# The FFN's up-projection in two Strassen parts: 512 tokens as before, then 2 x 1024 tokens through half-size products of 512 columns

## The chip, the core and the metric

The kernel runs on one core of one Trainium2 chip. A core has five engines, each with an instruction queue of its own that is worked off in order: TensorE (PE in the profile; its weight loads PEld), VectorE (DVE), ScalarE (ACT), GpSimd (POOL) and SyncE (SP, which here issues nearly all DMAs). They meet through semaphores. On-chip data lie in SBUF, matmuls write to PSUM, which has eight banks of 128 x 512 f32. The metric is the device time of one execution in microseconds, the median of several runs.

## The reference, cut

One layer of a bidirectional encoder in f32, for two batches with the same weights: a sample S of 2048 tokens and a prompt P of 512.

```
h = RMSNorm(x); p = h @ w_in
A: windowed attention   B: centred pooling   C: Hyena (FFT convolution)
x = x + concat(RMSNorm_A(a), RMSNorm_B(b), RMSNorm_C(c)) @ w_out
x = x + ConvGLU(RMSNorm(x)):
    u = h @ w_ffn_in                 # 1024 -> 2 x 2816
    u = depthwise conv of width 3 along the tokens + bias
    x += (gelu(u[:2816]) * u[2816:]) @ w_ffn_out
```

The change is in the first line of the ConvGLU, and in what is put beside it.

## The kernel before, in words

Each f32 product is made of three matmuls of rounded parts: `split` (L316) makes a high part on ACT (L318) and the rest on DVE (L319), and `mm3` (L321) multiplies high with high, high with low, low with high into one PSUM bank (L323, L324, L325). Activations are kept transposed, with features on the partitions, so the moving operand of the up-projection is 512 tokens of normed input (`h`, or `hp` for P) and the stationary one a 128 x 128 piece of weights (`fwhi`, `fwlo`).

`run` (L1433) builds the program from two generators at a time: `drive` takes steps of a main chain and of a side chain in a ratio of their estimated PE costs. That fixes each engine's order, up to a list scheduler beneath that keeps every engine's queue in order of readiness as it models it. The side chain is one sequence: mixers of S (spectra, pooling, Hyena, attention), the normed and transposed input of S's first half (`norm_s`), then, once the main chain has begun the up-projection (`need("up")`), attention, pooling, Hyena and output projection of P, and `prep_p`, P's normed input. Main chain: the input projections and S's output projection (`front`), then

- `ffn_in(S, hA, 0, 1024)`, beside the side chain at `RATIO_P` = 0.4,
- `ffn_in(P, hp, 0, 512)`, beside `ffn_prep` of S's second half,
- `ffn_in(S, hB, 1024, 1024)`, beside the first eight weight tiles of the down-projection (`load`),
- `ffn_out`, which reads the products back from DRAM and loads the other 14 weight tiles.

`ffn_in` (L1286) goes over 22 feature tiles x 2 parts (gate and up). Per tile: a 512 KB weight load (`fw`, two buffers), its split (ACT and DVE, 1024 columns each), then 8 k x 3 matmuls per 512 tokens, an ACT copy with tap 1 and bias from PSUM (L1322), two DVE taps from PSUM (L1312), and at the gate a Gelu (L1338). DVE multiplies gate and up (L1340), SP stores the 128 rows (`acts`, `actp`). `ffn_prep` loads 128 tokens (`nx`, two buffers), takes Square with a sum on ACT (L343), the power -1/2 on POOL (L346), the scaling on DVE (L347), eight PE transposes (L357), and splits them from PSUM on ACT and DVE (L360, L361).

Of the kernel before, what the change touches and what calls it, by code (L numbers as in the profile page):

```python
# [18 lines left out]
DM = 1024  # L19
# [13 lines left out]
class Seq:  # L33
    """One request batch: its length, its FFT split N = 64 * N2 and the derived tile counts."""
# [15 lines left out]
# the tables of 128 partitions that stay on chip: name and columns  # L50
# [5 lines left out]
def _shape_tables():  # L56
    """DFT matrices, positions, decays, distances: all from shapes alone."""
# [40 lines left out]
    # of the first four heads; those of the others are 1/16 of it  # L98
# [14 lines left out]
    for s in SEQS.values():  # L113
# [34 lines left out]
        # rows (b, ri, g, j), columns (ri, g, k2), block diagonal over g  # L148
# [13 lines left out]
        # positions of the forward filter and of the backward one, in the order (j, b, n1)  # L162
# [15 lines left out]
        # [b, n1, chunk, g, j, c']  # L178
# [15 lines left out]
def _arrays(inputs):  # L194
    """The arrays of the launch: the large inputs as they are, the small ones laid out by partition."""
# [35 lines left out]
RATIO_P = 0.4  # L231
# [10 lines left out]
class Trunk:  # L242
    def __init__(self, ctx, tc, d):
# [3 lines left out]
        for s in SEQS.values():  # L247
# [6 lines left out]
            self.act[n] = self.dr.tile([D_FF, s.L], F32, name="act" + n)  # L254

    def consts(self, c):
# [12 lines left out]
        self.edge = c.tile([128, 2, 2 * NF], F32, name="edge")  # L269
# [46 lines left out]
    def split(self, x, hi, lo):  # L316
        nc = self.nc
        self.keep(nc.scalar.activation(hi, x, AF.Copy))  # L318
        self.keep(nc.vector.tensor_tensor(lo, x, hi, op=ALU.subtract))  # L319

    def mm3(self, ps, lhi, llo, rhi, rlo, start, stop):  # L321
        nc = self.nc
        nc.tensor.matmul(ps, lhsT=lhi, rhs=rhi, start=start, stop=False)  # L323
        nc.tensor.matmul(ps, lhsT=lhi, rhs=rlo, start=False, stop=False)  # L324
        nc.tensor.matmul(ps, lhsT=llo, rhs=rhi, start=False, stop=stop)  # L325

    def row(self, pool, src, name):
        """A vector of DM on every partition."""
# [9 lines left out]
    def norm(self, pool, g, x, n):  # L338
        """The first n rows of x after RMS norm with gain g, in place."""
# [10 lines left out]
    def norm_t(self, xn, n, hi, lo, c0, bank):  # L350
        """xn, transposed, to columns c0.. of hi and lo."""
# [13 lines left out]
    def front(self):  # L365
        """p of the sample, q, k and v of both, p of the prompt, then the sample's output projection behind its attention. The
        weights of a part take the place of those of the part before, tile by tile."""
# [5 lines left out]
        with tc.tile_pool(name="front", bufs=1, reuse_waits="tile") as pool:  # L373
# [16 lines left out]
            def fill(i, c0):  # L390
                """Weights i: columns c0.. of w_in, piece by piece."""
# [30 lines left out]
            def place(i):  # L422
                """Where row tile i goes, transposed: hi, lo and the column."""
# [32 lines left out]
            def also(it):  # L456
                """it, with the row tiles and the weights to come."""
# [54 lines left out]
            # the first tiles as they come; the weights last, for the next pool to start below them  # L512
# [55 lines left out]
            def out_fill(k, dst):  # L568
                """Row tile k of the scaled w_out into dst [128, 2, DM]."""
# [57 lines left out]
            def rest():  # L627
                """The weights to come."""
# [24 lines left out]
    def filt_sin(self, pool, ps, li, x):  # L653
        """sin's argument f * (ps + b) into x, reduced to [-pi, pi]."""
# [905 lines left out]
```

## Time and profile before

| | us |
|---|---|
| median of 3 runs | 3138.26 (3133.56 to 3141.27) |
| span of the profiled execution | 3140.1 |
| first to last up-projection matmul | 1144.9 to 2531.3 |
| of these the stage with P | 1783.8 to 2036.4 |
| landing of a weight tile (`fw`, 512 KB, 132 of them) | 3.8 |
| ACT split of it / DVE split of it | 1.06 / 1.22 |

A row of a group reads: line, engine, operation, out<-in, shapes, count, then busy us and mean ns of one, then the engine's idle time just before and what ended it. A row of a tile gives minimum, median and maximum in ns, then when the first and the last began. A row of a stretch gives begin and end, its length, busy us (and count) of PE, PEld, DVE, ACT and POOL, the granted share of TensorE's clock, the share of the DMA engines and GB/s. A DMA row gives the count, KB each and median us from issue to landing. A timeline's row begins with start and duration in us. A matmul's duration of about 0.39 us includes its way through the array: they overlap, and one follows another in about 0.23 us.

### The profile page before, as it was taken

The page shows a single profiled execution, that of the slowest core. Times are in us where ns is not written, and L with a number is a line of the kernel's source. Part 1 is how long each engine was busy: PE and PEld are TensorE (multiplying, and loading weights), DVE is VectorE, ACT ScalarE, POOL GpSimd, SP SyncE. Part 2 cuts the span into 40 slices and gives each one's busy share as a digit, 9 for nine tenths or more (in the row PEclk, how much of TensorE's full clock was granted, in tenths as well). Part 3 has the DMA queues.
Part 4 walks back from the last instruction along what each step waited for, and adds up shares of the span by engine and source line. Part 5 has one row for each costly group of instructions (what it writes and reads, how often), then busy time and mean ns, then how long its engine had stood idle before and what let it go on. Part 6 is the DMA issues. An engine that isn't in the chain of part 4 may idle for free.

```text
span 3140.1 us, 41553 instructions
## 1 busy us (share of the span) xinstructions
PE 3053.5 (97%) x15992; PEld 2556.1 (81%) x15992; DVE 1676.3 (53%) x3168; ACT 1173.7 (37%) x2021; POOL 210.5 (7%) x248
## 2 busy tenths in 40 slices
PE   7999999899999999999999999999999999999999
PEld 6887888888878877788887888888888888888887
DVE  7443567759998777666445565564444442111111
ACT  5222454448877546434223343332222231111110
POOL 1000000012233230000000000000000000000000
PEclk9999999999999999999999999999999999999999
DMA  5555586663533441454313243442222143223222
GB/s 178 151 152 138 163 230 170 178 176 100 152 100 94 145 138 61 131 166 133 98 63 128 89 137 118 127 142 67 74 67 74 54 131 111 74 77 101 74 75 77
DMA packets 399051, 369.94 MB, mean 118 GB/s; under 512 B 74937, under 2 KB 332857, under 8 KB 397829
## 3 DMA queue, kind: packets, MB, share of 16 engines
q1 hardware_dynamic: 395685, 356.64, 37.6%
q0 software_dynamic: 2880, 10.49, 0.8%
q8 instruction: 126, 2.06, 0.3%
q14 instruction: 72, 0.59, 0.1%
q10 hardware_dynamic: 288, 0.16, 0.0%
HBM read 278.08 MB, written 89.13 MB: 117 GB/s over the span
## 4 chain that ended last, share of the span: by engine, by line
PE 69%; DVE 5%; ACT 3%; DMA 2%; issue 1%; POOL 1%; SPq 0%; POOLq 0%; ACTq 0%; DVEq 0%
PE b L323 21%; PE b L325 21%; PE b L324 21%; PE b L1160 1%; PE b L1111 1%; ACT sb L1127 1%; PE b L1142 1%; PE b L1141 1%; PE b L865 1%; PE b L852 1%; DVE sb L1114 0%; PE b L357 0%; DVE nx L347 0%; DVE sb L1135 0%; DMA raw<-in_w_in_dram 0%
## 5 line engine op out<-in xcount | busy, mean ns | idle before, releaser
L323 PE MATMUL b<-h,fwhi 128*128 128x512 f32 x1408 | 562.5, 400 | 0.9 <-DVE x L1237 0.9
L325 PE MATMUL b<-h,fwlo 128*128 128x512 f32 x1408 | 560.0, 398 | 0.3 <-DVE fwlo L319 0.3
L324 PE MATMUL b<-h,fwhi 128*128 128x512 f32 x1408 | 559.0, 397 | 0.0
L1312 DVE SCALAR_TENSOR_TENSOR cv<-b,cst,cv 128x511 f32<-128x511 f32 (+1 forms) x616 | 351.8, 593 | 153.9 <-ACT cv L1322 147.3
L319 DVE TENSOR_TENSOR fwlo<-fw,fwhi 128x1024 fp32r<-128x1024 f32 x132 | 161.4, 1224 | 326.7 <-ACT fwhi L318 326.7
L325 PEld LDWEIGHTS b<-h,fwlo 128*128 128x128 f32 x1408 | 265.5, 189 | 64.5 <-DVE fwlo L319 0.8
L323 PEld LDWEIGHTS b<-h,fwhi 128*128 128x128 f32 x1408 | 265.8, 189 | 63.1 <-issue 1.8
L324 PEld LDWEIGHTS b<-h,fwhi 128*128 128x128 f32 x1408 | 265.7, 189 | 61.6
L319 DVE TENSOR_TENSOR al<-ar,ah 128x512 fp32r<-128x512 f32 x110 | 76.0, 691 | 420.4 <-ACT ah L318 420.4
L318 ACT ACTIVATE fwhi<-fw 128x1024 fp32r<-128x1024 f32 x132 | 139.8, 1059 | 387.9 <-PE b L324 385.1
L324 PE MATMUL b<-h,ah 128*128 128x512 f32 x640 | 249.2, 389 | 0.0
L323 PE MATMUL b<-h,ah 128*128 128x512 f32 x640 | 249.1, 389 | 0.0
L325 PE MATMUL b<-h,al 128*128 128x512 f32 x640 | 248.9, 389 | 0.0
L318 ACT ACTIVATE ah<-ar 128x512 fp32r<-128x512 f32 x110 | 69.4, 631 | 474.9 <-PE b L324 462.4
L1322 ACT ACTIVATE cv<-b,cst 128x512 f32<-128x512 f32 x220 | 169.2, 769 | 200.1 <-PE b L325 199.9
L323 PE MATMUL b<-W,h 128*128 128x256 f32 (+1 forms) x672 | 224.7, 334 | 2.1 <-ACT W L318 0.7
L324 PE MATMUL b<-W,h 128*128 128x256 f32 (+1 forms) x672 | 214.8, 320 | 0.7 <-DVE W L319 0.3
L325 PE MATMUL b<-W,h 128*128 128x256 f32 (+1 forms) x672 | 213.9, 318 | 0.0
L323 PE MATMUL b<-h,W 128*128 128x256 f32 x640 | 200.3, 313 | 3.4 <-ACT W L318 1.5
L325 PE MATMUL b<-h,W 128*128 128x256 f32 x640 | 184.5, 288 | 3.8 <-DVE W L319 3.8
L324 PE MATMUL b<-h,W 128*128 128x256 f32 x640 | 183.1, 286 | 0.0
L325 PEld LDWEIGHTS b<-h,al 128*128 128x128 f32 x640 | 120.1, 188 | 25.3 <-DVE al L319 0.2
(204 smaller groups left out, 5791.8 us busy)
## 6 DMA issues: line engine op xcount, KB each, us to landing
fw<-in_w_ffn_in_dram SPq DMA_DIRECT2D x132, 512.0 KB, 3.8
ar<-acts SPq DMA_DIRECT2D x88, 256.0 KB, 2.7
nx<-in_x_sample_dram SPq DMA_DIRECT2D x32, 512.0 KB, 4.4
tf<-in_t2f_s_dram SPq DMA_DIRECT2D x64, 256.0 KB, 3.3
acts<-cv SPq DMA_DIRECT2D x22, 512.5 KB, 2.6
raw<-in_w_in_dram SPq DMA_DIRECT2D x44, 256.0 KB, 3.1
rw<-in_w_ffn_out_dram SPq DMA_DIRECT2D x44, 256.0 KB, 2.7
acts<-cv SPq DMA_DIRECT2D x22, 511.5 KB, 3.1
```

What stands on the lines that cost most here:

```text
L318: self.keep(nc.scalar.activation(hi, x, AF.Copy))
L319: self.keep(nc.vector.tensor_tensor(lo, x, hi, op=ALU.subtract))
L323: nc.tensor.matmul(ps, lhsT=lhi, rhs=rhi, start=start, stop=False)
L324: nc.tensor.matmul(ps, lhsT=lhi, rhs=rlo, start=False, stop=False)
L325: nc.tensor.matmul(ps, lhsT=llo, rhs=rhi, start=False, stop=stop)
L852: nc.tensor.matmul(ps[:, i * C:i * C + C], lhsT=tf[:, i], rhs=x1[:, k0 + i], start=True, stop=True)
L865: nc.tensor.matmul(ps[:, i * C:i * C + C], lhsT=ti[:, i], rhs=t1[:, i * C:i * C + C], start=True, stop=True)
L1111: nc.tensor.matmul(ps[:, :nk], lhsT=qs[h][:, b * 128:b * 128 + 128], rhs=kk[:, ks], start=(i == 0), stop=(i == 1))
L1127: nc.scalar.activation(sc[h][:, :nk], sc[h][:, :nk], AF.Exp, bias=ng[:, h:h + 1], accum_out=den[:, h:h + 1])
L1141: nc.tensor.matmul(po, lhsT=v, rhs=phi, start=(i == 0), stop=False)
L1312: nc.vector.scalar_tensor_tensor(o, ps, taps[i], o if to is None else to, op0=ALU.mult, op1=ALU.add)
L1322: nc.scalar.activation(cv[:, a - o0:a - o0 + 512], ps, AF.Identity, scale=taps[1], bias=self.fcb[:, m:m + 1])
```

## The change

The sample's first 512 tokens go through the old scheme (`h0`, `ffn_in`). The other 2048 go in two parts: S 512 to 1535, and S 1536 to 2047 with all of P. In each part the product of a 256 x 1024 piece of weights (gate and up of one feature tile) and 1024 x 1024 tokens is seen as 2 x 2 blocks and made by the Winograd form of one Strassen step: seven products of half size instead of eight, each of 4 k x 3 matmuls of 512 columns.

- `ffn_sums` makes the seven token operands: per pair of 128-token tiles 16 transposes, copies and sums on ACT, DVE and POOL into one tile `o`, and one DMA of 1.83 MB in pieces of 512 bytes into the DRAM tensor `ops0` or `ops1`. It ends the side chain.
- `ffn_operands` reads a part's operands back, 1 MB each, through two stage buffers `st`, and splits each into `o0` to `o6`, the low part on DVE or, for every second one, POOL. These tiles have one buffer each.
- `ffn_in7` makes per feature four weight sums on POOL (`fs`), the splits `g1` to `g4` (`fk`, `fl`), and the seven products in the order of operands 0, 4, 5, 3, 1, 6, 2 into four banks; the fifth, sixth and seventh accumulate into banks that were read before. Sums between banks go through `p1`, `u2`, `u3` on ACT and DVE into `u`, and the convolution reads `u` in SBUF.
- Attention of P stands ahead of the up-projection, before `prep` of the first 512 tokens. `RATIO_P` is 1.0. The output projection of P runs in two halves of columns, and splits its input anew in each. All 22 weight tiles of the down-projection are loaded behind the last part.

```diff
-RATIO_P = 0.4
+RATIO_P = 1.0
...
+    def ffn_sums(self, dst, tiles, bank):
...
+                if i % 2 == 0:
+                    o = pool.tile([128, 7, 4, 128], F32, tag="o", name="o")
+                    for j in range(2):
+                        nc.scalar.activation(o[:, j], pv[j], AF.Copy)
+                else:
+                    nc.vector.tensor_tensor(o[:, 3], pv[0], o[:, 0], op=ALU.subtract)
+                    nc.vector.tensor_tensor(o[:, 4], pv[1], o[:, 3], op=ALU.subtract)
+                    nc.scalar.activation(o[:, 2], pv[1], AF.Copy)
+                    nc.gpsimd.tensor_tensor(o[:, 5], o[:, 4], o[:, 0], op=ALU.subtract)
+                    nc.gpsimd.tensor_tensor(o[:, 6], o[:, 1], o[:, 4], op=ALU.subtract)
+                    c = i // 2 * 128
+                    nc.sync.dma_start(out=dst[:, :, :, c:c + 128].rearrange("p o k t -> p (o k) t"), in_=o.rearrange("p o k t -> p (o k) t"))
...
+    def ffn_operands(self, pool, stage, src):
+        for i, op in enumerate((0, 4, 5, 3, 1, 6, 2)):
+            x = stage.tile([128, 4, FH], F32, tag="st", bufs=2, name="st")
+            self.nc.sync.dma_start(out=x, in_=src[:, op])
+            h[op] = pool.tile([128, 2, 4, FH], F32R, tag=f"o{op}", name=f"o{op}")
+            self.split(x, h[op][:, 0], h[op][:, 1], self.nc.gpsimd if i % 2 else None)
...
+    def ffn_in7(self, pool, h, parts, bank):
...
+            g1 = split(ws[0], "fk", 8)
+            nc.gpsimd.tensor_tensor(s12[:, 0:4], a21, a22, op=ALU.add)
+            nc.gpsimd.tensor_tensor(s12[:, 4:8], s12[:, 0:4], a11, op=ALU.subtract)
+            nc.gpsimd.tensor_tensor(s34[:, 0:4], a11, a21, op=ALU.subtract)
+            g2 = split(s12, "fk", 8)
+            nc.gpsimd.tensor_tensor(s34[:, 4:8], a12, s12[:, 4:8], op=ALU.subtract)
+            g3 = split(s34, "fk", 8)
+            g4 = split(a22, "fl", 2)
...
+            yield from product(pa, g1, 0, 0)
+            nc.scalar.activation(p1, pa, AF.Copy)
+            yield from product(pb, g2, 4, 4)
+            add(u2, pb, p1)
+            yield from product(pd, g3, 0, 5)
+            add(u3, pd, u2)
+            yield from product(pc, g2, 0, 3)
+            add(u[:, 1, to[1]], pc, u3)
+            yield from product(pa, g1, 4, 1, False)
+            nc.scalar.activation(u[:, 0, to[0]], pa, AF.Copy)
+            yield from product(pd, g4, 0, 6, False)
+            add(u[:, 1, to[0]], pd, u2)
+            yield from product(pc, g3, 4, 2, False)
+            add(u[:, 0, to[1]], pc, u2)
...
-                     self.mark("c", "s"), pace(RATIOS[2]), self.attention(S, *att), norm_s(), self.need("up"), self.attention(P, *att),
+                     self.mark("c", "s"), pace(RATIOS[2]), self.attention(S, *att), self.attention(P, *att), prep(), self.need("up"),
                      pooled(P, a), self.hyena(P, [[0, 1]], a), self.mark("cat", "p"),
-                     self.out_proj(P, a, d["x_p"][0], "cat"), prep_p())
+                     self.out_proj(P, a, d["x_p"][0], "cat"), sums(0), sums(1))
...
+            for i, parts in enumerate(([(S, 512, 1024)], [(S, 1536, 512), (P, 0, 512)])):
+                h = self.ffn_operands(hops, stage, self.ops[i])
+                self.drive(self.ffn_in7(pool, h, parts, fb), None, 0)
```

What this does to the queues shows at three places. The first is PE at the beginning of the up-projection. Before, its matmuls (lines L323 to L325) follow on one another, and attention of P (here L1072, transposes of its keys) is woven in later:

```order
5470 L324 MATMUL b1_12336<-h_11694,fwhi_12269 128x512
5471 L325 MATMUL b1_12336<-h_11694,fwlo_12270 128x512
5472 L1072 MATMUL b6_12349<-cst_75,kn_12301 128x128 x4
5473 L323 MATMUL b1_12336<-h_11694,fwhi_12269 128x512
5474 L324 MATMUL b1_12336<-h_11694,fwhi_12269 128x512
```

After, the last attention products of P (L1144, L1145) stand ahead of the transposes of the four normed tiles (L360), and these ahead of the first up-projection matmul (L326):

```order
5615 L1144 MATMUL b7_12800<-phi_12806,v1_11701 128x512
5616 L1145 MATMUL b7_12800<-plo_12807,v1_11701 128x512
5617 L360 MATMUL b5_12847<-cst_77,nx_12829 128x128 x4
5619 L360 MATMUL b7_12870<-cst_77,nx_12838 128x128 x4
5621 L360 MATMUL b4_12893<-cst_77,nx_12861 128x128 x4
5623 L360 MATMUL b6_12907<-cst_77,nx_12884 128x128 x4
5625 L326 MATMUL b0_12932<-h00_12822,fwhi_12927 128x512
```

So attention and the normed tiles now come first, with no up-projection matmul between them. The second place is PE at the end of the first 512 tokens, after the change: the last matmul of `ffn_in`, the transposes for the sums (L1329, three pairs of tiles), and the first product of a Strassen part.

```order
6958 L328 MATMUL b3_15998<-h00_12822,fwlo_15994 128x512
6959 L1329 MATMUL b6_15697<-cst_77,nx_15622 128x128 x4
6961 L1329 MATMUL b4_15719<-cst_77,nx_15647 128x128 x4
6963 L1329 MATMUL b6_15784<-cst_77,nx_15710 128x128 x4
6965 L1329 MATMUL b4_15806<-cst_77,nx_15735 128x128 x4
6967 L1329 MATMUL b6_15872<-cst_77,nx_15797 128x128 x4
6969 L1329 MATMUL b4_15885<-cst_77,nx_15822 128x128 x4
6971 L326 MATMUL b0_16106<-o0_16043,fk_16082 128x512
```

Before, at the end of the first stage, the matmuls of S (`h`) and of P (`hp`) stand back to back:

```order
7996 L324 MATMUL b3_17018<-h_11694,fwhi_16985 128x512
7997 L325 MATMUL b3_17018<-h_11694,fwlo_16986 128x512
7998 L323 MATMUL b0_17060<-hp0_16169,fwhi_17055 128x512
7999 L324 MATMUL b0_17060<-hp1_16170,fwhi_17055 128x512
```

The third place is DVE inside a part, one feature after the change: the split of the next weights (L321), four taps of the feature before (L1436), and between them the sums (L1400) that the products of this feature wait for, in the order in which they stand.

```order
2314 L321 TENSOR_TENSOR fk_18429<-fw_18422,fk_18428 128x1024
2315 L1436 SCALAR_TENSOR_TENSOR cv_18273<-u_18172,cst_77,cv_18273 128x1024
2316 L1436 SCALAR_TENSOR_TENSOR cv_18278<-u_18172,cst_77,cv_18278 128x1024
2317 L1436 SCALAR_TENSOR_TENSOR cv_18273<-u_18172,cst_77,cv_18273 128x1024
2318 L1436 SCALAR_TENSOR_TENSOR cv_18278<-u_18172,cst_77,cv_18278 128x1024
2319 L1400 TENSOR_TENSOR u2_18312<-b1_18315,u1_18311 128x512
2320 L1441 TENSOR_TENSOR cv_18273<-cv_18273,cv_18278 128x1024
2321 L1400 TENSOR_TENSOR u3_18313<-b2_18316,u2_18312 128x512
2322 L1400 TENSOR_TENSOR u_18310<-b3_18317,u3_18313 128x512
2323 L321 TENSOR_TENSOR fk_18436<-fs_18426,fk_18435 128x1024
2324 L321 TENSOR_TENSOR fk_18441<-fs_18427,fk_18440 128x1024
2325 L1400 TENSOR_TENSOR u_18310<-b2_18316,u2_18312 128x512
```

Before, DVE's rows of a feature are one split and taps that read PSUM, and no matmul accumulates onto a bank that DVE has read.

More of the change, by code (lines that the diff above doesn't have):

```diff
@@ L230 @@
 RATIOS = (1.0, 1.2, 0.8)
-RATIO_P = 0.4
+RATIO_P = 1.0
+FH = 512
 CAP = 2000
@@ L254, in __init__ @@
             self.act[n] = self.dr.tile([D_FF, s.L], F32, name="act" + n)
+        self.ops = [self.dr.tile([128, 7, 4, FH], F32, name=f"ops{i}") for i in range(2)]
     def consts(self, c):
@@ L1256, in out_proj @@
-            yield from self.need((key, n))
-            for t in range(L // 128):
-                ts = slice(t * 128, t * 128 + 128)
-                ca = pool.tile([128, DM], F32, tag="ca", name="ca").rearrange("p (k t) -> p k t", k=KD)
-                nc.sync.dma_start(out=ca, in_=self.cat[n][:, ts].rearrange("(k p) t -> p k t", p=128))
-                x = pool.tile([128, DM], F32, tag="ox", name="ox")
-                nc.sync.dma_start(out=x, in_=src[ts, :])
-                sq, hi, lo = (pool.tile([128, KD, 128], dt, tag=nm, name=nm) for nm, dt in (("osq", F32), ("chi", F32R), ("clo", F32R)))
-                self.out_prep(ca, sq, hi, lo)
-                yield from self.until(self.now + T_NORM)
-                r = self.out_scale(pool, bank, sq, GROUPS)
-                yield from self.out_product(bank, hi, lo, x, r, GROUPS, wo)
-                nc.gpsimd.dma_start(out=self.x2[n][t * 128:t * 128 + 128, :], in_=x)
-                self.done.add(("x2", n, t))
@@ L1272, in ffn_prep @@
-    def ffn_prep(self, s, side, hs, h0, h1, bank):
-        n = s.name
-        hi, lo = hs
-        with self.tc.tile_pool(name=f"ffp{n}{h0}", bufs=2, side=side, reuse_waits="tile") as pool:
-            g2 = self.row(pool, self.d["norm2_g"][0], "g2")
-            t, last = h0, None
-            while t < h1 or last:
-                nxt = None
-                if t < h1:
-                    e = min(h1, t // 128 * 128 + 128)
-                    yield from self.need(("x2", n, t // 128))
-                    nxt = (self.norm(pool, g2, self.norm_load(pool, self.x2[n][t:e, :], e - t, 2), e - t), e - t, hi, lo, t - h0, bank), self.now + T_NORM
-                    t = e
-                if last:
-                    yield from self.until(last[1])
-                    yield from self.norm_t(*last[0])
-                last = nxt
@@ new lines, in prep_rows @@
+    def prep_rows(self, pool, tiles):
+        g2 = self.row(pool, self.d["norm2_g"][0], "g2")
+        box = []
+        for i in range(len(tiles) + 1):
+            if i < len(tiles):
+                n, t = tiles[i]
+                yield from self.need(("x2", n, t // 128))
+                x = self.norm(pool, g2, self.norm_load(pool, self.x2[n][t:t + 128, :], 128, 2), 128)
+                box.append((x, self.now + T_NORM))
+            if i:
+                x, t = box.pop(0)
+                yield from self.until(t)
+                yield x
@@ new lines, in ffn_prep @@
+    def ffn_prep(self, tiles, hi, lo, bank):
+        with self.tc.tile_pool(name="ffp", bufs=1, side="right", reuse_waits="tile") as pool:
+            i = 0
+            for x in self.prep_rows(pool, tiles):
+                if x is None or isinstance(x, (int, float)):
+                    yield x
+                    continue
+                yield from self.norm_t(x, 128, hi, lo, i * 128, bank)
+                i += 1
+    def ffn_sums(self, dst, tiles, bank):
+        nc = self.nc
+        with self.tc.tile_pool(name="ffs", bufs=1, side="right", reuse_waits="tile") as pool:
+            i, o = 0, None
+            for x in self.prep_rows(pool, tiles):
+                if x is None or isinstance(x, (int, float)):
+                    yield x
+                    continue
+                pv = []
+                for k0 in range(0, KD, 4):
+                    ps = bank()
+                    for k in range(k0, k0 + 4):
+                        nc.tensor.transpose(ps[:, (k - k0) * 128:(k - k0) * 128 + 128], x[:, 128 * k:128 * k + 128], self.ident)
+                    pv.append(ps.rearrange("p (k t) -> p k t", k=4))
+                    yield 450
+                if i % 2 == 0:
[10 more added lines that the diff above has]
+                    nc.sync.dma_start(out=dst[:, :, :, c:c + 128].rearrange("p o k t -> p (o k) t"), in_=o.rearrange("p o k t -> p (o k) t"))
+                i += 1
@@ L1531, in run, with raw @@
+        self.wo = {}
+        with tc.tile_pool(name="ffo", bufs=1, side="right", reuse_waits="tile") as po, tc.tile_pool(name="wo", bufs=1, reuse_waits="tile") as pw:
+            def raw():
+                return po.tile([128, 512], F32, tag="rw", bufs=2, name="rw")
+            for f in range(NF):
                 self.wo_load(pw.tile([128, 2, DM], F32R, name=f"wo{f}"), f, raw)
```

228 lines of the change are left out of this document (131 added, 97 removed).

## The prediction

> **What bounds the kernel now.** I read the page's busy shares first, then its chain of work, then the table of stages.
>
> ```profile
> PE 3053.5 (97%) x15992; PEld 2556.1 (81%) x15992; DVE 1676.3 (53%) x3168; ACT 1173.7 (37%) x2021; POOL 210.5 (7%) x248
> PE 69%; DVE 5%; ACT 3%; DMA 2%; issue 1%; POOL 1%; SPq 0%; POOLq 0%; ACTq 0%; DVEq 0%
> L323 PE MATMUL b<-h,fwhi 128*128 128x512 f32 x1408 | 562.5, 400 | 0.9 <-DVE x L1237 0.9
> 1145.00:1780.00 635.00, 627.56 (x2924) 510.87 (x2925) 374.38 (x757) 249.00 (x386) 37.20 (x43) 0.99 0.36 110
> 2037.00:2532.00 495.00, 495.00 (x2115) 397.94 (x2114) 239.20 (x432) 142.29 (x170) 0.00 (x0) 1.00 0.24 79
> L323 PE MATMUL b<-h,fwhi x1408: 388/397/774, 1144.9 to 2531.3; 128*128 128x512 f32 x176
> ```
>
> TensorE carries the end: 97% busy, 69% of the chain. The last row puts the up-projection at 1144.9 to 2531.3 us; in its first stage (columns: length, PE, PEld, DVE, ACT, POOL, clock, DMA share, GB/s) PE is idle 635 - 627.56 = 7.4 us, in its last one not at all. So every matmul removed there is worth its whole pitch, and every new wait that PE meets costs its whole length. The question is which of the two is larger.
>
> **The gain.** Before: 44 feature tiles x 5 token blocks x 8 k x 3 = 5280 matmuls of 512 columns. After: 44 x 8 x 3 = 1056 for the first 512 tokens, and 2 parts x 22 features x 7 products x 4 k x 3 = 3696. That is 528 fewer.
>
> ```profile
> 1900.00:2000.00 100.00, 100.00 (x430) 80.48 (x429) 52.87 (x63) 36.78 (x45) 0.00 (x0) 1.00 0.39 119
> 2050.00:2150.00 100.00, 100.00 (x428) 80.40 (x427) 53.65 (x97) 33.81 (x44) 0.00 (x0) 1.00 0.34 109
> 2700.00:2800.00 100.00, 100.00 (x438) 82.03 (x437) 17.82 (x26) 11.38 (x18) 0.00 (x0) 1.00 0.27 90
> ```
>
> 100 / 428 gives a pitch of 0.2336 us, so **-123 us**. If the 3696 ran at the 100 / 438 = 0.2283 of the down-projection, another 20 would go; I don't count on it, as the new parts keep the other engines busier than any up-projection stage here.
>
> **Front.** Attention of P moves ahead of the up-projection. Behind its last product stand only transposes of four normed tiles and then the first up-projection matmul, which needs all of `h00`.
>
> ```profile
> L1142 PE MATMUL b<-plo,v x20: 391/397/481, 1184.5 to 1284.3; 128*128 128x512 f32 x20
> 600.00:1050.00 450.00, 423.64 (x2677) 369.09 (x2676) 384.65 (x958) 319.51 (x730) 118.80 (x120) 1.00 0.42 123
> nx<-x2s SPq DMA_DIRECT2D x16, 512.0 KB, 4.8
> g<-in_norm_g_dram SPq DMA_DIRECT2D x4, 512.0 KB, 5.7
> L343 ACT ACTIVATE nsq<-nx 128x1024 f32<-128x1024 f32 x12 | 12.7, 1055 | 11.5 <-DMA nx<-x2s 10.0 <-POOL rr L346 1.3 <-DMA nx<-x2p 0.2
> L346 POOL TENSOR_TENSOR rr<-ss,mhalf x60: 539/549/1528, 6.2 to 1855.2; 128x1 f32<-128x1 f32 x60
> L347 DVE SCALAR_TENSOR_TENSOR nx<-nx,rr,g 128x1024 f32<-128x1024 f32 x12 | 15.4, 1286 | 6.3 <-POOL rr L346 6.1
> L360 ACT ACTIVATE h<-b 128x512 fp32r<-128x512 f32 x16 | 9.3, 591 | 18.0 <-PE b L357 18.0
> L361 DVE TENSOR_TENSOR h<-b,h 128x512 fp32r<-128x512 f32 x16 | 10.9, 685 | 1.1 <-ACT h L360 1.0
> ```
>
> SP issues these loads behind the last attention store and a weight load that waits for a split queued behind the last output (about 3 us). `nx` has two buffers, so two rounds: gain row 5.7 (tile 4.8 in the second), two Squares 2.1, pow 0.55, product 1.29, transposes and evacuation about 2.5: 12 + 11. Idle 3 + 23 = 26. Attention of S left PE idle 26.4 of 450 us, 5.9%; P's took 1284 - 1145 = 139 us under the matmuls, so some 8 more. **+34** (25 to 50).
>
> **Hyena and output projection of P** now stand beside half the matmuls they had.
>
> ```profile
> L795 SPq DMA_DIRECT2D hst<-pTp x6: 326/327/384, 1305.5 to 1405.8; - x6
> L941 ACT ACTIVATE hst<-b x2: 1082/1092/1101, 1435.6 to 1438.8; 128x512 f32<-128x512 f32 x2
> ```
>
> The chain took about 120 us from its first matmul behind the 1305.5 load to 1435.6; the order leaves it PE rows worth some 95. What is short shows as waits; some is in the 7.4 already. **+19** (8 to 40).
>
> **Tail of the sums.** The main part's last matmul stands ahead of twelve groups of transposes, three pairs of tiles. The operand tile `o` has one buffer, so a pair cannot be evacuated until the pair before is in DRAM.
>
> ```profile
> q1 hardware_dynamic: 395685, 356.64, 37.6%
> L1054 POOL TENSOR_TENSOR kn<-kt,hr 128x512 f32<-128x512 f32 x2 | 2.1, 1041 | 0.2
> cats<-ob SPq DMA_DIRECT2D x32, 128.0 KB, 2.5
> ```
>
> A write has 3584 pieces of 512 bytes. The queue row gives 0.376 x 16 x 3140.1 / 395685 = 47.7 ns a packet on an engine, so 3584 / 16 x 0.0477 = 10.7 us; the nearest row, a store of equally small rows, says at least 2.5. I take 8.5, nearer the first. Cycle: copies 1.2 and subtractions 1.4 by the rows of `h`, POOL's two 2.1, write 8.5, hops 1: 14. Two whole cycles and the last pair's 4 to 6: **+34** (19 to 45).
>
> **Operands.** 7 loads of 1 MB per part through two stage buffers, each split by ACT and then DVE or POOL.
>
> ```profile
> hst<-pTs SPq DMA_DIRECT2D x6, 1024.0 KB, 7.1
> cats<-hst SPq DMA_DIRECT2D x2, 1024.0 KB, 4.7
> L319 DVE TENSOR_TENSOR fwlo<-fw,fwhi 128x1024 fp32r<-128x1024 f32 x132 | 161.4, 1224 | 326.7 <-ACT fwhi L318 326.7
> ```
>
> The first two loads go early; each later one waits for the split two ahead. With splits of 2.1 + 2.4 us (two 1024-wide ones; on POOL 2 + 3.9) the seventh operand is ready 33 (loads of 4.7) to 39 us (7.1) after the tail, where the products alone need it at 17: **+19** at the first part (14 to 25). At the second the first part's last feature covers most: **+5** (0 to 12).
>
> **Start of the down-projection.** Eight weight tiles were loaded under the last part; now all 22 follow it, and their splits stand behind the last feature's convolution on ACT and DVE: four Identities, taps, Gelu, product, then two splits. **+10** (5 to 15).
>
> ```profile
> L1322 ACT ACTIVATE cv<-b,cst 128x512 f32<-128x512 f32 x132 | 101.3, 767 | 86.8 <-PE b L325 86.6
> L802 DVE SCALAR_TENSOR_TENSOR hst<-hst,mcst 128x512 f32<-128x512 f32 x12 | 8.8, 737 | 3.8 <-ACT hst L799 3.6
> L1254 DVE SCALAR_TENSOR_TENSOR owlo<-raw,cst,owhi 128x1024 fp32r<-128x1024 f32 x8 | 10.2, 1280 | 2.9 <-ACT owhi L1253 2.9
> ```
>
> **Inside the parts.** A feature is 84 matmuls, 19.6 us of PE. DVE per feature: splits 3 x 1.22 + 0.69, five sums of 0.69, four taps of 1.28, one product 1.22: 14.0 us; eight 0.74 us taps in the second part make it 14.8. ACT has about 9, POOL 4 x 1.04. So PE would bound, but POOL and DVE hinder each other here:
>
> ```profile
> 718.06 1.90 POOL L1059 TENSOR_TENSOR qn<-qt,hr 128x1024 f32<-128x1024 f32 x1
> 718.82 1.16 DVE L1129 TENSOR_TENSOR den<-den,es 128x4 f32<-128x4 f32 x1
> L1129 DVE TENSOR_TENSOR den<-den,es x31: 149/161/1862, 713.7 to 1044.3; 128x4 f32<-128x4 f32 x31
> ```
>
> The DVE operation, 0.16 us at its median, ends when POOL's does. The new POOL sums start about 2.4 us into a feature, when its next weights land, and meet the taps, which read SBUF only: 2.3 + 4 x 1.28 + 4 x 1.04 = 11.6; then `u2`, the product, `u3`: 14.2. Product 6 accumulates into the bank that `u3` reads, and is due after five products, 14.0. In the second part taps end 0.8 later. So 0.2 and 1.0 us a feature, at most 22 x 1.2 = 26; where the two overlap less, nothing. I take **+15** (0 to 45, if each feature loses 1).
>
> The Trainium skill (SBUF — State Buffer, "Who interferes with whom") calls the pair of ports "an exclusive lock" against DVE operations with two SBUF inputs, and says that one in PSUM doesn't contend. By it the taps and splits block in full and the sums `u2`, `u3` never do, and the term would be the 26 just worked out; the row of `den` agrees, and no row here shows a tap under a POOL sum.
>
> **At nothing.** The weights: 132 tiles of 512 KB in both kernels, two a feature in 19.6 us, 54 GB/s and their 3.8 us landing (the `fw` row of the page's DMA issues) lie under PE, as 79 GB/s do in the last stage; without that cover, were a tile asked for only when needed, 3.8 x 44 = 167 us. The PSUM copies and edges on ACT lie under the products: a feature takes four of the eight banks, so the next one's can start. If that failed, a copy of 0.6 a feature would show, 26 us.
>
> **Clock.**
>
> ```profile
> 360.00:365.00 5.00, 3.58 (x19) 2.33 (x18) 2.63 (x6) 2.32 (x4) 0.00 (x0) 1.00 0.65 193
> 365.00:370.00 5.00, 5.00 (x25) 3.88 (x26) 4.42 (x10) 2.57 (x5) 0.00 (x0) 0.66 0.72 177
> 1330.00:1335.00 5.00, 5.00 (x29) 4.90 (x29) 2.95 (x5) 1.66 (x3) 0.00 (x0) 0.62 0.35 106
> 1335.00:1340.00 5.00, 5.00 (x23) 4.14 (x22) 4.01 (x9) 0.70 (x2) 0.00 (x0) 0.70 0.77 199
> ```
>
> After PE idles 1.4 us the clock is 0.66 for 5 us: 1.7 us lost; the second spell lost 1.9 + 1.5. Five new pauses after which PE runs dense: **+8** (0 to 20). The Trainium skill (TensorE: Matmul & The Clock Gate, "What's actually happening") has the half clock follow an idle window of some 3.4 us and last as long; by its figure an estimate of 1.7 for each of five is 8.5. The trace is harsher: it throttled after a shorter pause.
>
> **Sum.** -123 - 7 + 34 + 19 + 34 + 19 + 5 + 10 + 15 + 8 = **+14**. The profiled execution's span is 3140.1, the median 1.8 lower: 3140.1 + 14 - 1.8 = **3152**.
>
> **Rivals.** *The sums keep up (not slower).* If the write of a pair takes the 2.5 us of the small store's row, a cycle is about 8; eight cycles are 64 us, which fit beside the main part, no transposes are late, and the 34 go: 3118. For it: DMA engines are 36% busy in this stage. Against: 14 times the pieces of that store, and the order puts three pairs behind the last matmul whatever the write takes. It decides at a cycle below some 9 us. *DVE and POOL bound the parts.* If the lock delays also product 7 and the splits, each feature takes 1.5 us more, 66 instead of 15: 3203. For it: 14.8 + 4.2 = 19.0 of 19.6 us and single `u` buffers. Against: only the four POOL sums block. It decides when `u3` comes past 14 us in the first part too. *The saving isn't there:* the order shows the 4752 matmuls, so only the pitch could; at 0.2283 it is 20 larger, 3132.
>
> **Numbers.** Measurement tells 0.3%, 9.4 us, from no change. Forecast 0.45 (3152, its own range 3127 to 3177): 0.02 faster, 0.16 same, 0.27 slower. Sums keep up 0.25: 0.18 faster, 0.07 same. DVE and POOL 0.2, all slower. Higher pitch and others 0.1: 0.06 faster, 0.04 slower. Together faster 0.26, same 0.23, slower 0.51. The range reaches from the sums' rival with the small lock, less 15 (3100), to the DVE one and 7 more (3210).
>
> **What would show it.** A gap of some 25 us with `nx` loads before the first `fwhi` matmul; transposes 14 us apart behind the last one; products of the first feature 5 to 6 us apart; in the steady parts, 19.6 to 20.6 us a feature with PE waiting for `u3`. Wrong, if the features take 19.6 with no wait, if one term is twice its value, or if PE's pitch in the parts isn't 0.2336.

## The result, and the profile after

The changed kernel takes **3177.5 us** (3175.3 to 3178.1), the one before 3137.3 in the same comparison: a ratio of **1.0125**, 95% interval 1.0111 to 1.014. It is slower by 39 us where 14 were forecast: the direction was right and the time lies within the full range of 3100 to 3210 and at the very end of the forecast's own 3127 to 3177; the size is off by 25 us.

The profiled execution has a span of 3176.3 us, 36.2 more than before. The page's first line, and the line of its chain of work:

```profile
PE 2977.4 (94%) x15488; PEld 2475.9 (78%) x15488; DVE 1944.5 (61%) x3162; ACT 1320.5 (42%) x2235; POOL 596.8 (19%) x470
PE 47%; DMA 4%; DVE 2%; issue 1%; ACT 1%; POOL 1%; SPq 0%; DVEq 0%; POOLq 0%; ACTq 0%
```

PE's busy time fell by 76 us, and not by the 123 that 528 matmuls are worth; its idle time rose from 86.6 to 198.9, by 112. 112 - 76 = 36. Both halves have to be explained. Where the idle time lies shows in the table of stretches of the changed kernel (begin and end, length, busy us of PE, PEld, DVE, ACT, POOL, clock, DMA share, GB/s):

```profile
1047.00:1207.00 160.00, 126.90 (x639) 102.89 (x639) 112.19 (x274) 84.83 (x189) 40.00 (x49) 0.90 0.37 114
1207.00:1500.00 293.00, 287.57 (x1397) 236.54 (x1396) 188.57 (x316) 123.78 (x166) 30.43 (x49) 1.00 0.57 171
1500.00:1634.00 134.00, 84.73 (x385) 67.94 (x383) 71.46 (x101) 55.47 (x87) 42.65 (x39) 0.82 0.80 233
1634.00:1725.00 91.00, 75.40 (x284) 57.02 (x285) 57.85 (x44) 35.86 (x39) 34.90 (x15) 0.92 0.43 142
1725.00:2075.00 350.00, 350.00 (x1502) 281.73 (x1501) 305.23 (x252) 153.34 (x199) 155.22 (x71) 1.00 0.25 82
2075.00:2140.00 65.00, 49.47 (x191) 38.80 (x190) 59.59 (x47) 30.42 (x31) 33.23 (x12) 0.89 0.40 130
2140.00:2542.00 402.00, 402.00 (x1724) 323.54 (x1723) 289.44 (x428) 183.95 (x245) 117.53 (x80) 1.00 0.25 79
2542.00:2640.00 98.00, 89.30 (x363) 68.71 (x362) 42.00 (x63) 36.26 (x60) 0.00 (x0) 0.97 0.53 165
```

Length less PE: 33 us idle at the front, 5 beside Hyena and output projection of P, 49 at the sums, 16 while the first operands arrive, 16 where the second part's replace them, 9 at the start of the down-projection, and none in the two long stretches in which the products run. The first of these was 9.3 over the corresponding stretches before (4.3 up to 1145, 5.0 beside P's attention). The clock column is below 1 only in stretches with idle time, and in all of those with over 8 us of it.

PE's longest waits between 1626 and 2545 us, from the end of the sums to the down-projection, say who was late (waiting instruction, whom it waited for, us in total, times, longest):

```profile
PE b L326 <- ACT o L320: 12.1, 3, 7.9
PE b L326 <- DVE u L1400: 11.5, 3, 5.6
PE b L327 <- DVE o L321: 8.6, 2, 7.7
PE b L327 <- POOL o L321: 3.9, 3, 2.5
```

### The profile page after: what moved, and what is told of

Its sections match the earlier page's. It is cut to its first block, busy times and chain, and to the rows that moved or that the text cites. A ratio compares the mean times of both kernels' runs of the same rounds, so it can differ in the third digit from the quotient of the medians.

```text
span 3176.3 us, 41398 instructions
## 1 busy us (share of the span) xinstructions
PE 2977.4 (94%) x15488; PEld 2475.9 (78%) x15488; DVE 1944.5 (61%) x3162; ACT 1320.5 (42%) x2235; POOL 596.8 (19%) x470
## 4 chain that ended last, share of the span: by engine, by line
PE 47%; DMA 4%; DVE 2%; issue 1%; ACT 1%; POOL 1%; SPq 0%; DVEq 0%; POOLq 0%; ACTq 0%
PE b L328 16%; PE b L326 16%; PE b L327 16%; DMA rw<-in_w_ffn_out_dram 2%; DVE cv L1436 1%; DMA st<-ops 1%; DMA raw<-in_w_out_dram 1%; DMA ops<-o 1%; DMA fw<-in_w_ffn_in_dram 0%; POOL o L321 0%; DVE wo L321 0%; DMA nx<-x2s 0%; ACT wo L320 0%; DVE cv L1441 0%; PE b L1329 0%
## 5 line engine op out<-in xcount | busy, mean ns | idle before, releaser
L326 PE MATMUL b<-o,fk 128*128 128x512 f32 x1056 | 419.7, 398 | 12.5 <-ACT o L320 12.1
L327 PE MATMUL b<-o,fk 128*128 128x512 f32 x1056 | 419.9, 398 | 10.1 <-DVE o L321 8.6
L328 PE MATMUL b<-o,fk 128*128 128x512 f32 x1056 | 419.0, 397 | 0.0
L326 PE MATMUL b<-wo,ah 128*128 128x512 f32 x880 | 349.2, 397 | 7.8 <-ACT wo L320 6.9
L327 PE MATMUL b<-wo,ah 128*128 128x512 f32 x880 | 348.7, 396 | 0.8 <-DVE wo L321 0.8
L328 PE MATMUL b<-wo,al 128*128 128x512 f32 x880 | 348.8, 396 | 0.3
L321 DVE TENSOR_TENSOR al<-ar,ah 128x512 fp32r<-128x512 f32 x110 | 75.8, 691 | 406.2 <-ACT ah L320 406.2
L1436 DVE SCALAR_TENSOR_TENSOR cv<-u,cst,cv 128x1024 f32<-128x1024 f32 (+2 forms) x264 | 308.4, 1208 | 11.5 <-ACT cv L1434 7.7
L326 PEld LDWEIGHTS b<-o,fk 128*128 128x128 f32 x1056 | 199.7, 189 | 62.7 <-ACT o L320 13.6
L327 PEld LDWEIGHTS b<-o,fk 128*128 128x128 f32 x1056 | 199.8, 189 | 61.0 <-DVE o L321 10.6
L328 PEld LDWEIGHTS b<-o,fk 128*128 128x128 f32 x1056 | 199.4, 189 | 47.9
L1400 DVE TENSOR_TENSOR u<-b,u 128x512 f32<-128x512 f32 x220 | 151.2, 687 | 132.2 <-PE b L328 129.3
L326 PE MATMUL b<-W,h 128*128 128x256 f32 (+1 forms) x672 | 225.6, 336 | 1.4 <-ACT o L510 0.6
L326 PEld LDWEIGHTS b<-wo,ah 128*128 128x128 f32 x880 | 165.5, 188 | 50.5 <-ACT wo L320 7.8
L326 PE MATMUL b<-h,W 128*128 128x256 f32 x640 | 200.7, 314 | 3.5 <-ACT W L320 1.6
L328 PEld LDWEIGHTS b<-wo,al 128*128 128x128 f32 x880 | 165.5, 188 | 42.5 <-DVE al L321 2.3
L327 PEld LDWEIGHTS b<-wo,ah 128*128 128x128 f32 x880 | 165.5, 188 | 41.8 <-DVE wo L321 1.6
L328 PE MATMUL b<-h,W 128*128 128x256 f32 x640 | 184.6, 288 | 2.8 <-DVE W L321 2.8
L1389 POOL TENSOR_TENSOR fs<-fw 128x512 f32<-128x512 f32 x44 | 89.3, 2029 | 505.1 <-DMA fw<-in_w_ffn_in_dram 333.7
```

The lines of the kernel that those rows point to most:

```text
L321: self.keep((engine or nc.vector).tensor_tensor(lo, x, hi.bitcast(F32), op=ALU.subtract))
L1389: nc.gpsimd.tensor_tensor(s12[:, 0:4], a21, a22, op=ALU.add)
L1400: nc.vector.tensor_tensor(o, ps, x, op=ALU.add)
L1436: nc.vector.scalar_tensor_tensor(o, u[:, part, c + i - 1:c + i - 1 + k], self.fcw[:, i, m:m + 1], o, op0=ALU.mult, op1=ALU.add)
```

## The experiments

Theory after the result: the steady products cost what was worked out, and the surplus is made of the seams between stages (the sums' tail, the two arrivals of operands) and of two things that slow PE itself: the clock after idle time, and a longer pitch in the down-projection, a stage that the change only meant to feed differently. From start to start a matmul of that stage took 0.2287 us on average before and 0.2333 after: 2640 x 0.0046 = 12 us. Rival: everything is the waits, and the pitch follows from them. Each run was timed beside the kernel before; ratios are to that, so they can be compared across chips.

### The pitch: 32 bytes ahead of the down-projection's weights

In the kernel before, the weight tiles of 16 of the 22 features lay in upper pools and ran at 0.227 us, the other six at 0.233. After the change all 22 lie in one lower pool.

```diff
+            nc.gpsimd.memset(pw.tile([128, 8], F32, name="pad"), 0.0)
             for f in range(NF):
                 self.wo_load(pw.tile([128, 2, DM], F32R, name=f"wo{f}"), f, raw)
```

> A 32-byte tile ahead of the down-projection's weight tiles moves these to addresses that are 32 modulo 64, where the stationary operands (ah, al) already lie. Theory: a matmul follows the one before in 0.2268 us where both operands have the same address modulo 64 and in 0.2333 where they differ; in the kernel before, 16 of the 22 weight tiles lay so, after the change none. Then the 2640 matmuls of this stage go from 0.2333 to 0.2268 and the time falls by 17 us, to about 3160. Rival: what counts is in which part of SBUF the tiles lie (the 16 fast ones stood in the upper pools); then nothing changes, 3177.

Measured: ratio 1.0093 (1.0078 to 1.0108), 3163.1 us. The pitch became 0.2290, between the two. A pad changed it, so the pool isn't what counts; but equality modulo 64 alone doesn't give the 0.2268.

### The same for the parts' weights

```diff
+            nc.gpsimd.memset(pool.tile([128, 8], F32, name="pad"), 0.0)
             for i, parts in enumerate(([(S, 512, 1024)], [(S, 1536, 512), (P, 0, 512)])):
```

> The same 32 bytes ahead of the split weights of the two Strassen parts, so that they lie as the operands o0 to o6 do modulo 64. Theory: the 3696 matmuls go from 0.2333 to 0.2268 us, 24 us less, about 3153. Rival, that only the place in SBUF counts or that DVE and POOL (17.5 of 20 us busy on DVE) bind as soon as a feature of 84 matmuls takes 19.05 us: nothing, or less than half of it, 3165 to 3177.

Measured: ratio 1.0112 (1.0086 to 1.0138), no change that could be told. The parts stayed at 0.2333 us. Equality modulo 64 alone is refuted.

### Equality modulo 512 in both stages

The two pads with 56 columns (224 bytes) in place of 8.

> 224 bytes ahead of the parts' split weights and 224 ahead of the down-projection's weight tiles, so that in both stages stationary and moving operand have the same address modulo 512, as the 16 fast tiles of the kernel before had. Theory: that equality, and not the one modulo 64 alone, gives the 0.2268 us; then the 3696 and the 2640 matmuls lose 0.0065 each, 41 us, about 3136. Rival: it worked in the down-projection for another reason (32 bytes gave 0.2290 there and nothing in the parts); then the down-projection alone changes, by 10 to 17 us, 3160 to 3167, and the parts stay at 0.2333.

Measured: **0.9993** (0.9984 to 1.0003), 3135.0 us: 41 less than the change, as the theory had it. Two stretches of 100 us, one in a part, one in the down-projection, first of the changed kernel, then of this one:

```profile
1900.00:2000.00 100.00, 100.00 (x431) 80.50 (x430) 87.44 (x71) 42.45 (x55) 46.56 (x22) 1.00 0.25 79
2700.00:2800.00 100.00, 100.00 (x430) 80.34 (x429) 15.84 (x23) 11.41 (x18) 0.00 (x0) 1.00 0.21 67
```

```profile
1900.00:2000.00 100.00, 100.00 (x443) 82.84 (x442) 88.07 (x74) 45.76 (x59) 43.64 (x21) 1.00 0.27 85
2700.00:2800.00 100.00, 100.00 (x443) 82.83 (x442) 18.10 (x27) 11.38 (x18) 0.00 (x0) 1.00 0.28 92
```

12 and 13 matmuls more in 100 us, with PE busy throughout in all four. (These rows count each matmul that reaches into the stretch, one or two too many; so the prediction's 0.2336 from 428 was 0.2343 from start to start.)

### Which distance counts

A pad of 32 bytes ahead of every one of the 22 weight tiles, so that one execution shows sixteen distances between moving (`wo`) and stationary operand (`ah`, `al`).

```diff
             for f in range(NF):
+                nc.gpsimd.memset(pw.tile([128, 8], F32, name=f"pad{f}"), 0.0)
                 self.wo_load(pw.tile([128, 2, DM], F32R, name=f"wo{f}"), f, raw)
```

> 32 bytes ahead of every weight tile of the down-projection, so that the 22 tiles lie at steps of 32 bytes against ah and al modulo 512 (wo6 at 0, wo7 at 32, up to wo21 at 480, and wo0 to wo5 at 320 to 480). Read from the pitch of each tile's matmuls. Theory: only equality modulo 512 (wo6) gives 0.2268 and all others 0.2333. Rival A: a smaller modulus does, 64 or 128: then every second or fourth tile is fast. Rival B: the distance counts by degrees, with tiles near equality in between.

Measured, as the mean from start to start over 88 pairs of each tile in the units of 256 tokens after the second (distance: address of the moving operand less that of the stationary one):

```
distance modulo 256     0      32      64      96     128     160     192     224
tiles 6 to 13, us    .2272   .2336   .2297   .2345   .2336   .2338   .2326   .2326
tiles 14 to 19, us   .2272   .2336   .2297   .2345   .2336   .2338
```

Tiles 0 to 5, at distances of 64 to 224, agree with the table within 0.0002. Tiles 20 and 21, whose matmuls alternate, ran at 0.2312 and aren't in it; why they differ stays open. None of the three statements was right in full: what counts is the distance modulo **256**, with a second, lesser dip at 64. The table fits the other stages within 0.001 us: the pad of 32 bytes had put the down-projection at a distance of 64 (0.2290 measured) and left the parts at 192 (0.2333), the change has 32 (down-projection) and 224 (parts), the kernel before 0 for sixteen tiles of its down-projection (0.2268). The addresses are those that the allocator gave; the trace doesn't show them. What in the chip makes it so wasn't tried.

### The kernel before, with such pads

Pads of 416 bytes ahead of the up-projection's weights, of `hp`, and of the last six weight tiles of the down-projection.

> The kernel before with pads of 416 bytes ahead of its up-projection weights, hp and the last six down-projection weight tiles, so that stationary and moving operands agree modulo 512 everywhere in the FFN. Theory: 5280 matmuls from 0.2343 to 0.2268, 40 us, and 720 by 0.0066, 5: ratio 0.986, 3092; the change, padded likewise (0.9993), then stands 1.3% behind it, as unpadded, and the pitch is no merit or fault of Strassen's step. Rival: the up-projection here is held by something else at 0.2343 (evacuation from PSUM, weights): less than half, 0.993 or more.

Measured: **0.9895** (0.9876 to 0.9915), 3101.6 us; the pitch of its steady up-projection is 0.2267. The gain is 35 of the 45 expected: in the first stage, where the up-projection is woven with side work, its pitch was 0.2339 to begin with and became 0.2286. So the slow pitch is no trait of Strassen's step. Padded, the change stands 0.9993 to 0.9895, 1.0% behind, where unpadded it is 1.25% behind. Its first 512 tokens had no pad in that run; by the pitch that they reached with one in the kernels below (0.228 after 0.234, 1056 matmuls) I estimate 6 us more, and 0.8%. Placement thus explains some 12 to 14 of the 39 us that the change costs.

### Without POOL in the parts

```diff
-            self.split(x, h[op][:, 0], h[op][:, 1], self.nc.gpsimd if i % 2 else None)
+            self.split(x, h[op][:, 0], h[op][:, 1])
...
-            nc.gpsimd.tensor_tensor(s12[:, 0:4], a21, a22, op=ALU.add)
+            nc.vector.tensor_tensor(s12[:, 0:4], a21, a22, op=ALU.add)
```

and likewise for the other three sums of the weights. Sums and low parts moved in one run; what each is worth alone wasn't tried.

> The four weight sums of a feature and all low parts of the operands on DVE, nothing on POOL in the parts. Theory: POOL and DVE hold one another up (a 512-wide sum on POOL takes 2.0 to 2.3 us there and not 1.04, four taps 11.2 and not 5.1), which costs nothing while the products run, but at the change of parts the taps are late and with them the operands; without POOL some 8 to 15 us of the 21 lost there and 2 to 5 of those at the first operands go: 3160 to 3169. Rival: all seven low parts in one queue are later than with POOL's help, or DVE binds the steady parts (14.0 + 4 x 0.69 = 16.8 of 19.6 us): 3177 to 3190.

Measured: 1.0042 (1.0028 to 1.0056), 3150.7 us; **26 less** than the change, more than the theory gave. The groups of DVE and POOL in the parts, of the changed kernel:

```profile
L1436 DVE SCALAR_TENSOR_TENSOR cv<-u,cst,cv 128x1024 f32<-128x1024 f32 x88 | 182.1, 2129 | 2.9 <-ACT cv L1434 1.5
L1389 POOL TENSOR_TENSOR fs<-fw 128x512 f32<-128x512 f32 x42 | 86.8, 2066 | 505.1 <-DMA fw<-in_w_ffn_in_dram 333.7 <-DVE u L1400 134.5 <-DVE fk L321 21.0
L321 POOL TENSOR_TENSOR o<-st,o 128x2048 fp32r<-128x2048 f32 x6 | 30.8, 5140 | 32.3 <-ACT o L320 20.0 <-ACT edge L1423 12.3
L1400 DVE TENSOR_TENSOR u<-b,u 128x512 f32<-128x512 f32 x219 | 150.5, 687 | 132.1 <-PE b L328 129.3 <-DVE u L1400 0.5
```

and without POOL, where the sum of 512 columns is one of 42 on DVE:

```profile
L1436 DVE SCALAR_TENSOR_TENSOR cv<-u,cst,cv 128x1024 f32<-128x1024 f32 x88 | 107.1, 1278 | 0.0
L1389 DVE TENSOR_TENSOR fs<-fw 128x512 f32<-128x512 f32 x42 | 28.9, 688 | 3.5 <-DMA fw<-in_w_ffn_in_dram 2.8
L1400 DVE TENSOR_TENSOR u<-b,u 128x512 f32<-128x512 f32 x219 | 150.4, 687 | 79.1 <-PE b L328 78.7
1637.00:1683.00 46.00, 39.99 (x146) 30.22 (x147) 27.50 (x21) 19.55 (x17) 0.72 (x1) 0.85 0.61 212
2050.00:2110.00 60.00, 55.05 (x222) 42.06 (x221) 53.29 (x56) 33.57 (x35) 0.00 (x0) 0.97 0.47 149
```

Side by side, a tap of 1024 columns took 2.13 us and a POOL sum 2.07; apart, the tap takes 1.28 and the sum, on DVE, 0.69. This is the first part: in its steady stretch every tap ran beside a POOL sum, which took 2.14 to 2.28 there. In the second part's steady stretch no tap did, and the taps of 512 and 513 columns take 0.75 us in both kernels. The sums `u` from PSUM take 0.687 either way, also those that ran beside a POOL sum (0.68 to 0.69). In the steady stretches this was hidden (PE 350.00 of 350). At the seams it wasn't: the last two rows are the arrival of the first operands (6 us idle, then none; 16 with POOL) and of the second (5 us; 16). Together that is some 20 us of idle time; PE's busy time fell by 5.6, of which half clock explains at most 2.3. At the second seam the longest pair of the changed kernel is the last product of gate and up (L1441, 1.2 us where it ran alone) beside the low part of an operand, which POOL makes in 4.7 to 6.6 us and DVE in 2.3:

```profile
2116.38 5.59 DVE L1441 TENSOR_TENSOR cv<-cv 128x1024 f32<-128x1024 f32 x1
2115.36 5.54 POOL L321 TENSOR_TENSOR o<-st,o 128x2048 fp32r<-128x2048 f32 x1 [1.05 <-ACT o L320]
```

### Attention of P back behind the beginning of the up-projection

```diff
-                     ... self.attention(S, *att), self.attention(P, *att), prep(), self.need("up"),
+                     ... self.attention(S, *att), prep(), self.need("up"), self.attention(P, *att),
```

> Attention of P back behind the beginning of the up-projection, with the rest as in the change. Theory: the side chain is long by its latencies, and beside 512 tokens there is no room for another 139 us of it: the waits at the front (24 us) go, but 28 of the 32 groups of transposes for the sums then stand behind the last matmul, and at 15 us a pair the tail grows by 60 or so: 3200 to 3230. Rival: attention fills the gaps of the other side work, and the 24 us are simply gained: 3145 to 3160.

Measured: 1.019 (1.0175 to 1.0205), 3197.1 us: 20 slower than the change, in the theory's direction, at somewhat over half of what its 60 less 24 come to, and just short of its range. The up-projection begins 66 us sooner and its first stage ends 42 sooner, but the tail until the first product of a part is long:

```profile
1544.00:1657.00 113.00, 27.69 (x116) 22.07 (x114) 41.03 (x53) 34.94 (x59) 40.67 (x38) 0.54 0.74 223
```

85 us of idle PE. So moving attention ahead was the better order here: it costs less at the front than behind.

### The order at the sums' tail

`RATIO_P = 2.0` in place of 1.0.

> RATIO_P from 1.0 to 2.0: the side chain gets twice the share beside the first 512 tokens, so that 28 of the 32 groups of transposes for the sums stand ahead of the last up-projection matmul of this stage (20 before). Theory: the tail is a matter of order, about 49 us of waits around it, and most of it goes: 20 to 35 us less, 3142 to 3157. Rival: the side chain is bound by its own latencies (loads, norms, the write of each pair), and the waits only move in between the matmuls: within 6 us of 3177.

Measured: 1.0063 (1.0048 to 1.0078), 3153.0 us; by the ratios 19 to 20 less: the theory, at its lower end. From the first up-projection matmul to the first product of a part it takes 408.7 us, 427.9 in the change.

### Two buffers for the operand tile

```diff
-                    o = pool.tile([128, 7, 4, 128], F32, tag="o", name="o")
+                    o = pool.tile([128, 7, 4, 128], F32, tag="o", bufs=2, name="o")
```

> Two buffers for the operand tile o of the sums. Theory: the copy of the next pair waits for the DMA of the pair before (8.6 us, seen three times in the tail), and a pair's cycle of 15 to 21 us falls below 10: 12 to 20 us less, 3157 to 3165. Rival: the loads and norms of the pair's tiles, whose Square stands behind those copies, set the cycle by themselves: less than 5 us, 3172 to 3177.

Measured: 1.0075 (1.0058 to 1.0092), 3158.3 us; by the ratios 16 less, as the theory said. In the changed kernel PE waited for the normed tiles before the transposes for the sums (L1329), and ACT for the write before its copies of the next pair (us, times):

```profile
PE b L1329 <- DVE nx L350: 22.1, 7, 11.6
PE b L1329 <- DVE ss L347: 19.3, 4, 9.8
  DMA ops<-o: 17.6, 4
```

With two buffers the last row no longer appears, and the first two are 9.4 and 8.7.

### Four buffers for the normed tiles

`norm_load(..., 128, 4)` in place of 2 in `prep_rows`.

> Four buffers for the tiles that are normed (nx) in prep and sums, two before. Theory: the four tiles ahead of the first up-projection matmul then load in one round, and the second round of load and Square, about 8 to 10 us, goes from the front: 3163 to 3169, ratio 1.008 to 1.010. Rival: the loads wait in SP's queue behind other loads, or the norm chain is one after the other on ACT anyway: less than 3 us, 3174 or more.

Measured: 1.0091 (1.0075 to 1.0107), 3164.1 us. The size was forecast, the place wasn't: from the last attention product to the first up-projection matmul it takes 28.4 us against 31.2, so 3 at the front, and from there to the first product of a part 416.1 against 427.9, so 12 beyond it. The longest wait at the front is the same in both, before the first transposes; of the changed kernel:

```profile
PE b L360 <- DVE ss L347: 17.5, 1, 17.5
1182.62 0.37 SPq L1454 DMA_DIRECT2D fw<-in_w_ffn_in_dram  x1
1183.66 13.75 SPq L338 DMA_DIRECT2D nx<-x2s  x4
```

The last attention product began at 1175.2. SP issues the first `nx` load at 1183.7, behind a weight load that waits for a split: eight of the 17.5 us are its queue, which more buffers don't shorten.

### Together

Two buffers, ratio 2.0 and the 32-byte pad:

> Two o buffers, RATIO_P 2.0 and the 32-byte pad ahead of the down-projection's weights together. The ratio alone gave a ratio to the kernel before of 1.0063, two buffers 1.0075, the pad 1.0093, the change 1.0125. Theory: the first two work on the same tail of about 49 us of waits and overlap, the pad is independent: 20 + 8 + 10 less, a ratio of about 1.000, 3137 against a before of 3137. Rival: the tail's waits are gone with either one; then 20 + 10, 1.003.

Measured: 1.0053 (1.0037 to 1.0069), 3153.3 us, short of the rival too. The order now has every transpose ahead of the stage's last matmul, and the stage itself waits: in it PE is idle

```profile
1212.00:1622.00 410.00, 375.23 (x1782) 304.00 (x1781) 251.00 (x409) 173.19 (x245) 58.80 (x80) 0.96 0.65 196
```

35 of 410 us. From the first up-projection matmul to the first product of a part the profiled execution (3160.6 us) takes 427.7 us, as in the change (427.9), while the pad kept its worth (0.2292 us in the down-projection). By the ratios both cures gave 12 us over the pad alone (1.0093), less than either by itself: two cures of one tail don't add up.

No POOL in the parts, pads in all three FFN stages, and the ratio:

> No POOL in the parts, the 224-byte pads in both parts and down-projection, a 416-byte pad ahead of the weights of the first 512 tokens (so that they too agree with h00, h01 modulo 512), and RATIO_P 2.0. Theory: four places, each its own, so the ratios add up: 1.0125 - 0.0083 - 0.0132 - 0.0062, and 1056 x 0.0075 = 8 us, 0.0025, for the new pad: 0.982, 3081. Rival: as with two buffers and ratio together, what is gained at the tail comes back as waits within; then 0.988, 3100.

Measured: 0.9858 (0.9842 to 0.9874), 3091.0 us, between the two. The same with two `o` buffers in place of the ratio:

> As the one before with two o buffers in place of the ratio: 1.0125 - 0.0083 - 0.0132 - 0.0050 - 0.0025 = 0.9835, 3086. Rival: 0.988 or more.

Measured: **0.9853** (0.9837 to 0.9869), **3089.3 us**: faster than the kernel before by 1.5%, and than the padded kernel before (3101.6, timed with it) by 0.4%. Its page begins

```profile
PE 2920.7 (95%) x15488; PEld 2465.0 (80%) x15488; DVE 1960.2 (64%) x3344; ACT 1319.6 (43%) x2235; POOL 241.9 (8%) x291
```

And that with four `nx` buffers as well:

> The kernel with two o buffers, no POOL in the parts and the pads (0.9853), and four nx buffers, with which all transposes for the sums stand ahead of the last matmul of the first 512 tokens. Theory: another 3 us at the front and some 5 at the tail: 0.983, 3081. Rival: as with two buffers and the ratio together, the waits move to within the stage: 0.985 to 0.987.

Measured: 0.9866 (0.985 to 0.9883), 3095.9 us: the rival. From the first up-projection matmul to the first product of a part it takes 418.5 us, against 406.8 without the four buffers.

## Why the prediction was right in direction and wrong in size

- **The gain, -123.** It came as reckoned. The 528 matmuls went, and the steady parts ran without a wait: 350.00 of 350 and 402.00 of 402 us busy, 0.2333 us from start to start.
- **Front, +34.** Idle time of 33 against 9 before: 24. The gap behind the last attention product holds 23 of it, where 26 were reckoned: the part that is SP's order (8 us) was taken as 3, the second round of loads was shorter. The 8 for the waits of P's attention did not come: 10.0 us idle up to its end, 9.3 before.
- **Hyena and output projection, +19.** 5.4 idle in 293 us against 1.8 in the corresponding 370: some 4. The chain found room in the denser order.
- **Tail of the sums, +34.** 49. Behind the stage's last matmul PE idled 37, near the 34, but from other lengths: the write landed in 8.6 us, as taken, the cycles were 22 and 16 us, not 14, because the next Square stands behind the copy that waits for the write, and PE's own transposes filled 11. The other 12 lie ahead of that matmul, where the first wait came 78 us before it; the sum had none there. Both cures found 16 to 20 us here. The rival in which the sums keep up was wrong.
- **Operands, +19 and +5.** 16 and 16. The second was mis-sized: the reload was reckoned with splits of their own length, and there DVE's work for the last feature and POOL's low parts hold one another up; without POOL the two seams showed 6 and 5.
- **Inside the parts, +15.** Zero where it was put: in the steady features `u3` ended 13.2 us into a feature, 0.8 ahead of the need, and not 14.2; in the second part 9.3. That taps and sums hold one another up was right (2.13 us a tap, 2.07 a sum), the place wrong. Its cost fell on the seams, and taking POOL out, sums and low parts together, gave 26 us. The Trainium skill's exclusive lock (SBUF — State Buffer, "Who interferes with whom") agrees with the rows: beside POOL the taps, the products and, at the second seam, two splits of operands (2.8 and 3.4 us, 2.3 alone), all with two SBUF inputs, stretched, the sums from PSUM didn't. The term of 26 that followed from it for the steady features did not occur: the slack of a feature took it up.
- **Start of the down-projection, +10.** 9.
- **Clock, +8.** This failed. PE worked 68 us at half clock in the changed kernel, 14 before: up to 34 - 7 = 27 us lost. How much of the 27 the waits would have cost anyway wasn't isolated: no run held the clock up by itself. I counted one spell for each of five pauses; the clock came back and fell again within the same seam, and it stayed at half for 31 us at the front and 34 at the tail, where PE worked in short groups of matmuls:

```profile
1178.30:1209.00 30.70, 10.34 (x38) 8.41 (x39) 13.29 (x23) 10.80 (x18) 2.23 (x4) 0.50 0.48 153
1605.00:1639.00 34.00, 10.06 (x33) 7.48 (x34) 13.69 (x14) 13.25 (x17) 21.54 (x17) 0.50 0.71 199
```
- **Not in the sum at all: the down-projection's pitch, +12.** I read its 0.2283 as a property of that stage, "as the new parts keep the other engines busier than any up-projection stage here", and never asked why it was faster than the up-projection. The pads showed what it depends on, and that the busier engines have no part in it: padded parts ran at 0.2267 with DVE 88% busy.

The step that failed is the treatment of PE's own time as matmuls times a fixed pitch, with 8 us for the clock: busy time was to fall by 115 us (-123 + 8) and fell by 76. The matmuls' records, summed by stage, say where the 39 are. A matmul's time at half clock is counted here as half, and the other half stands in a row of its own:

| PE busy, us | before | after | difference | forecast |
|---|---|---|---|---|
| up-projection | 1236.2 | 1112.7 | -123.5 | -123 |
| down-projection | 604.0 | 619.0 | +15.0 | 0 |
| all other matmuls | 1206.5 | 1211.6 | +5.1 | 0 |
| half clock, at most | 6.8 | 34.2 | +27.3 | +8 |

So the clock beyond the 8 is 19, the down-projection 15 (12 of it pitch) and the rest 5, of which 2 are the sums of squares (`osq`) that P's output projection now makes twice. That the down-projection's share hangs on placement is shown by the pads; that the clock cost its whole 27 is not shown. The idle terms came to 112 against a forecast of 129 (all but gain and clock). That these are near one another is partly luck: single terms were off by up to 15 us, with both signs.

## What to carry to other kernels

A pitch that differs between two stages of the same matmul is a question to ask before a change moves tiles: here two pads of 224 bytes were worth as much as the change cost. When side work is in order and bound by latency, it can be cheaper to put it before the stage that needs it, as attention of P here, than behind; a smaller count of matmuls pays only if the seams that it adds are overlapped. Sums that "fit" on an idle POOL are not free when DVE reads two SBUF operands at the same time: reckon the pair as one engine wherever the slack ends.

## What the runs showed of the hardware that I had not expected

The spacing of 128 x 512 f32 matmuls depends on the address distance of their two SBUF operands modulo 256 bytes: 0.227 us at 0, 0.230 at 64, 0.2326 to 0.2345 at the other multiples of 32 (one execution; in four stages pads that bring it to 0 gave 0.227 to 0.228). In the steady first part four taps of DVE took 2.07 us each beside four sums of POOL of 2.14 to 2.28; alone they take 1.28 and 1.04, so that the pair (8.9 us) was hardly faster than one after the other (9.3). The clock stood at half for 34 us on end in which PE worked for 10.
